# GpSimd takes one row in four of an RMSNorm-SiLU normalization from VectorE

## The chip, the cores and the metric

The kernel runs on one core of a Trainium2 chip. The time is device microseconds (us) of one execution; a median is given with the lowest and highest execution. A *span* is the profiled execution, about 1.3 us shorter than the time. Ratios are the mean time of one kernel's fast runs over the mean of the other's fast runs of the same rounds, so not quite the ratio of the medians quoted beside them. An execution is called slow when it is more than 1.5% above the fastest of the same kernel.

## The reference

```python
# x: 16 x 1024 x 512 float32, gamma: 512 float32 (all ones here), eps 1e-5
rms = np.sqrt(np.mean(x ** 2, axis=-1, keepdims=True) + eps)
x_norm = x / rms * gamma
return x_norm * (1.0 / (1.0 + np.exp(-x_norm)))
```

The input is 33.55 MB and so is the output: 67.1 MB must go through the DMA once.

## The kernel before

The 16,384 rows lie 128 to a partition. A *unit* is four rows of each partition (1 MB in, 1 MB out), and there are 32. Loads are issued by SyncE into a ring of 96 rows per partition; stores are issued by ScalarE. For a unit, ScalarE squares three rows into PSUM and a fourth with a running sum, VectorE sums the three from PSUM, GpSimd makes 1/rms of four numbers per partition, VectorE multiplies each row by 1/rms and gamma in place, and ScalarE applies SiLU in place.

```python
for k in range(K):                                     # GpSimd, 32 units
    aeps[k] = ms[k] + eps          # tensor_scalar, 128x4, waits for the sums of unit k
    rstd[k] = aeps[k] ** -0.5      # tensor_tensor pow, 128x4, waits for aeps
...
def norm(k):                                           # VectorE
    _, at, _ = chunks[k]
    for j in range(cn):                                # cn = 4 rows
        row = xb[:, at + j, :]
        ins = nc.vector.scalar_tensor_tensor(
            out=row, in0=row, scalar=rstd[:, k, j : j + 1], in1=gamma_sb,
            op0=ALU.mult, op1=ALU.mult,
        )
        if j == 0:
            need(ins, s_rstd, k + 1)
    ins.then_inc(s_norm, 1)

for k in range(K + 1):                                 # VectorE's order:
    if k < K:
        sums(k)                                        # tensor_reduce from PSUM
    ...
    if k >= 1:
        norm(k - 1)
```

(The GpSimd loop is written short here; the cuts are marked.)

## Time and profile before

| what | before |
|---|---|
| time, median (lowest to highest) | 160.27 us (160.11 to 160.32) |
| span | 158.7 us |
| one unit in the steady part | 4.31 us |
| VectorE / ScalarE / GpSimd busy | 87% / 79% / 41% |
| DMA rate over the span | 423 GB/s |
| last store issued | 150.11 us |

Read it as two questions. What repeats, and what does one repeat wait for? And does something else stand behind it at nearly the same height? The chain that ended last answers the first only; the DMA in stretches answers the second. The lines themselves are in the prediction below, but for one, the normalizing row (line, operation, shapes, count, then busy us and mean ns of one):

```profile
L224 DVE SCALAR_TENSOR_TENSOR xb<-xb,rstd,gamma_sb 128x512 f32<-128x512 f32 x128 | 87.4, 748 | 0.0
```

### The profile page before, as it was taken

How to read it: one execution, taken by the hardware profiler on the slowest of the kernel's cores; microseconds unless marked ns; L12 is line 12 of the kernel's file. 1: busy time of each engine (PE TensorE's matmuls, PEld its weight loads, DVE VectorE, ACT ScalarE, POOL GpSimd, SP SyncE). 2: the span in 40 equal slices, each digit the busy share in tenths (PEclk: the TensorE clock that was granted, in tenths of full speed). 3: DMA queues.
4: the chain of work that ended last, by engine and by line, in shares of the span. 5: the costliest groups of instructions: out<-in, count | busy, mean ns of one | idle time of the engine just before them, and what ended most of it. 6: DMA issues, size and time to landing. Idle time of an engine off the chain costs nothing.

```text
span 158.7 us, 439 instructions
## 1 busy us (share of the span) xinstructions
DVE 138.9 (87%) x162; ACT 125.3 (79%) x129; POOL 65.4 (41%) x71
## 2 busy tenths in 40 slices
DVE  0249999999999999999999999999999999999300
ACT  0935989888888889988888888888998888883600
POOL 2035444444455555544444445555544444445000
DMA  7999999999999999999999999999999999999997
GB/s 235 427 523 405 396 450 419 409 452 407 460 394 413 467 421 452 413 396 479 432 413 429 446 429 413 425 417 458 429 454 396 434 446 438 446 413 438 388 458 301
DMA packets 3324, 67.15 MB, mean 423 GB/s; under 512 B 501, under 2 KB 501, under 8 KB 505
## 3 DMA queue, kind: packets, MB, share of 16 engines
q1 hardware_dynamic: 1584, 33.56, 49.9%
q10 hardware_dynamic: 1736, 33.57, 49.3%
q14 instruction: 4, 0.02, 0.0%
HBM read 33.56 MB, written 33.56 MB: 423 GB/s over the span
## 4 chain that ended last, share of the span: by engine, by line
DVE 85%; DMA 5%; ACT 1%; issue 1%; POOL 0%; POOLq 0%
DVE xb L224 53%; DVE ms L213 32%; DMA gamma<-in_gamma_dram 5%; ACT xb L184 1%; DVE gamma_sb L237 0%; POOL gamma L142 0%; POOL blank L141 0%; POOLq L65 0%
## 5 line engine op out<-in xcount | busy, mean ns | idle before, releaser
L224 DVE SCALAR_TENSOR_TENSOR xb<-xb,rstd,gamma_sb 128x512 f32<-128x512 f32 x128 | 87.4, 748 | 0.0
L184 ACT ACTIVATE xb<-xb 128x2048 f32<-128x2048 f32 x32 | 61.1, 1909 | 17.8 <-DVE xb L224 17.8
L213 DVE TENSOR_REDUCE ms<-sq 128x3 f32<-128x1536 f32 x32 | 56.1, 1754 | 7.0 <-ACT sq L172 7.0
L147 POOL TENSOR_SCALAR aeps<-ms 128x4 f32<-128x4 f32 x32 | 20.6, 644 | 75.2 <-DVE ms L213 75.2
L172 ACT ACTIVATE sq<-xb 128x1536 f32<-128x1536 f32 x32 | 45.9, 1433 | 0.0
L154 POOL TENSOR_TENSOR rstd<-aeps,neg_half 128x4 f32<-128x4 f32 x32 | 44.0, 1376 | 2.7
L165 ACT ACTIVATE junk<-xb 128x512 bf16<-128x512 f32 x32 | 19.7, 615 | 3.4 <-DMA xb<-in_x_dram 3.3
L165 ACT ACTIVATION_READ_ACCUMULATOR junk<-xb 128x1 f32 x32 | 6.0, 186 | 0.0
L199 ACT ACT_TABLE_LOAD x1 | 1.3, 1283 | 3.6 <-issue 3.6
L237 DVE LOAD_MASK_SELECT gamma_sb<-gamma x1 | 0.0, 14 | 2.3 <-DMA gamma<-in_gamma_dram 2.3
L141 POOL MEMSET blank<- 128x16 f32 x1 | 0.1, 111 | 1.5 <-POOLq L65 1.5
L237 DVE STREAM_SHUFFLE gamma_sb<-gamma 128x512 f32<-128x512 f32 x1 | 0.7, 717 | 0.0
L142 POOL MEMSET gamma<- 128x512 f32 x1 | 0.5, 524 | 0.0
L264 POOL MEMSET const-float32-0.0<- 128x1 f32 x1 | 0.1, 98 | 0.2 <-issue 0.2
L264 POOL MEMSET const-bfloat16-1.0<- 128x1 bf16 x1 | 0.1, 102 | 0.0
L264 POOL MEMSET const-uint8-127<- 128x1 uint8 x1 | 0.1, 101 | 0.0
L143 POOL MEMSET neg_half<- 128x4 f32 x1 | 0.1, 101 | 0.0
L264 POOL MEMSET const-float32-1.0<- 128x1 f32 x1 | 0.1, 98 | 0.0
## 6 DMA issues: line engine op xcount, KB each, us to landing
xb<-in_x_dram SPq DMA_DIRECT2D x6, 4096.0 KB, 41.9
out_dram<-xb ACTq DMA_DIRECT2D x6, 4096.0 KB, 31.1
xb<-in_x_dram SPq DMA_DIRECT2D x3, 2048.0 KB, 35.0
out_dram<-xb ACTq DMA_DIRECT2D x3, 2048.0 KB, 10.7
xb<-in_x_dram SPq DMA_DIRECT2D x2, 1024.0 KB, 5.8
out_dram<-xb ACTq DMA_DIRECT2D x2, 1024.0 KB, 20.8
scratch<-blank ACTq DMA_DIRECT2D x1, 8.0 KB, 7.7
gamma<-in_gamma_dram ACTq DMA_DIRECT2D x1, 8.0 KB
```

Source lines behind the costliest of these rows:

```text
L141: nc.gpsimd.memset(blank, 0.0).then_inc(s_blank, 1)
L142: nc.gpsimd.memset(gamma4, 0.0).then_inc(s_zero, 1)
L147: nc.gpsimd.tensor_scalar(out=aeps[:, k, :], in0=ms[:, k, :], scalar1=eps_f, scalar2=None, op0=ALU.add,),
L154: nc.gpsimd.tensor_tensor(out=rstd[:, k, :], in0=aeps[:, k, :], in1=neg_half, op=ALU.pow),
L165: acc = nc.scalar.activation(out=junk[k % 2], in_=xb[:, at + n_sq, :], func=AF.Square, scale=inv_d**0.5, accum_out=ms[:, k, n_sq : n_sq + 1],)
L172: square = nc.scalar.activation(out=sq[k % 2][:, 0:n_sq, :], in_=xb[:, at : at + n_sq, :], func=AF.Square, scale=inv_d**0.5,)
L184: nc.scalar.activation(out=rows, in_=rows, func=AF.Silu), s_norm, k + 1
L199: nc.scalar.preload_act_table_set("silu_and_others")
L213: nc.vector.tensor_reduce(out=ms[:, k, 0:n_sq], in_=sq[k % 2][:, 0:n_sq, :], op=ALU.add, axis=mybir.AxisListType.X,),
L224: ins = nc.vector.scalar_tensor_tensor(out=row, in0=row, scalar=rstd[:, k, j : j + 1], in1=gamma_sb, op0=ALU.mult, op1=ALU.mult,)
L237: nc.vector.stream_shuffle(gamma_sb, gamma4, [0] * 32), s_gld, 16
L264: nc = _bacc.Bacc("TRN2", target_bir_lowering=False, num_devices=1)
```

## The change

VectorE is busy without a gap and GpSimd is idle for half of the time. The change gives the fourth row of each unit to GpSimd. There it is done with two instructions, one multiply by 1/rms and one by gamma; ScalarE's SiLU waits for both engines. The core of the diff:

```diff
+    n_vec = 3
...
             s_eps, k + 1,
         ).then_inc(s_rstd, 1)
+        if k == 0:
+            nc.gpsimd.wait_ge(s_gamma, 1)
+        _, at, _ = chunks[k]
+        for j in range(n_vec, cn):
+            row = xb[:, at + j, :]
+            done = k * (cn - n_vec) + j - n_vec
+            need(
+                nc.gpsimd.tensor_scalar(
+                    out=row, in0=row, scalar1=rstd[:, k, j : j + 1], scalar2=None,
+                    op0=ALU.mult,
+                ),
+                s_rstd, k + 1,
+            ).then_inc(s_scaled, 1)
+            ins = need(
+                nc.gpsimd.tensor_tensor(out=row, in0=row, in1=gamma_sb, op=ALU.mult),
+                s_scaled, done + 1,
+            )
+        ins.then_inc(s_rest, 1)
...
     def swish(k):
+        nc.scalar.wait_ge(s_rest, k + 1)
...
     def norm(k):
-        for j in range(cn):
+        for j in range(n_vec):
```

More of the change, by code (lines that the diff above doesn't have):

```diff
@@ L95 @@
     s_norm = nc.alloc_semaphore("s_norm")
+    s_rest = nc.alloc_semaphore("s_rest")
+    s_scaled = nc.alloc_semaphore("s_scaled")
     s_swish = nc.alloc_semaphore("s_swish")
```

## The prediction

> **What bounds the kernel now.** I read the page's chain that ended last first, then the windows of DMA share, then the issue-to-landing times of the stores, then the timeline of one steady unit. A unit is four rows per partition, 1 MB in and 1 MB out; there are 32.
>
> ```profile
> DVE 138.9 (87%) x162; ACT 125.3 (79%) x129; POOL 65.4 (41%) x71
> ...
> DMA packets 3324, 67.15 MB, mean 423 GB/s; under 512 B 501, under 2 KB 501, under 8 KB 505
> ...
> DVE 85%; DMA 5%; ACT 1%; issue 1%; POOL 0%; POOLq 0%
> ```
>
> The chain says VectorE: 85% of the span is its two groups, with no idle time between them. Taken alone this promises that taking a quarter of the normalization away saves 32 x 0.66 us = 21 us. But the same page shows 423 GB/s over the whole span, so I looked at the DMA in stretches (columns: stretch and its length, VectorE, ScalarE and GpSimd busy us, clock, DMA share, GB/s):
>
> ```profile
> 4.00:12.00 8.00, 2.72 (x4) 5.04 (x7) 1.26 (x2) 1.00 1.12 471
> 40.00:60.00 20.00, 20.00 (x24) 17.73 (x20) 9.60 (x10) 1.00 1.00 421
> 80.00:100.00 20.00, 20.00 (x24) 17.73 (x19) 8.73 (x10) 1.00 1.01 434
> 120.00:130.00 10.00, 10.00 (x12) 9.10 (x9) 4.10 (x5) 1.00 1.02 441
> 150.00:154.00 4.00, 0.00 (x0) 0.08 (x1) 0.00 (x0) 1.00 1.00 430
> 154.00:158.70 4.70, 0.00 (x0) 0.00 (x0) 0.00 (x0) 1.00 0.77 331
> ```
>
> The DMA share is 1.00 from beginning to end, at about 430 GB/s in every stretch, whether loads and stores are mixed or (after some 110 us) only stores are left. At 430 GB/s the 67.15 MB take 156.2 us of the 158.7. So there are **two walls that stand almost at the same place**: VectorE, and the DMA behind it. Stores show the queue: a 4 MB store needs 31.1 us from issue to landing, though 4.19 MB at 430 GB/s are 9.8 us. At the end, the last silu ends at 150.08, the last store (2.1 MB) is issued at 150.11 and the span ends at 158.7, 8.6 us later. Alone it would take 4.9 us of moving and, by my estimate, some 2 us of issue and completion, 6.8 us. So some 1.8 us of backlog stood before it: the compute may end about 1.8 us later before the span feels it, and if it ends earlier the span gains next to nothing.
>
> One steady unit (start us, length, engine, line, operation), and the first pair of small GpSimd instructions, which ran while VectorE was idle:
>
> ```profile
> 8.87 0.23 POOL L147 TENSOR_SCALAR aeps<-ms 128x4 f32<-128x4 f32 x1 [6.36 <-DVE ms L213]
> 9.18 1.04 POOL L154 TENSOR_TENSOR rstd<-aeps,neg_half 128x4 f32<-128x4 f32 x1
> ...
> 59.11 1.75 DVE L213 TENSOR_REDUCE ms<-sq 128x3 f32<-128x1536 f32 x1
> 59.23 1.91 ACT L184 ACTIVATE xb<-xb 128x2048 f32<-128x2048 f32 x1 [0.45 <-DVE xb L224]
> 60.77 2.73 DVE L224 SCALAR_TENSOR_TENSOR xb<-xb,rstd,gamma_sb 128x512 f32<-128x512 f32 x4
> 60.95 0.66 POOL L147 TENSOR_SCALAR aeps<-ms 128x4 f32<-128x4 f32 x1 [2.19 <-DVE ms L213]
> ...
> 61.69 1.39 POOL L154 TENSOR_TENSOR rstd<-aeps,neg_half 128x4 f32<-128x4 f32 x1
> ```
>
> The unit repeats every 4.31 us: the reduce at 1.67 us of pitch and four normalizing instructions at 0.66 us each (2.65 us). ScalarE needs 1.82 + 0.61 + 1.44 = 3.87 us of it and waits 0.45 us. GpSimd is idle for 2.19 us per unit. The small GpSimd pair takes 0.23 and 1.04 us beside an idle VectorE, 0.66 and 1.39 us beside the normalization.
>
> **What the Trainium skill says, and whether the trace agrees.**
> SBUF — State Buffer, section "Who interferes with whom": VectorE and GpSimd share a read interface; a VectorE instruction with two SBUF inputs contends with a GpSimd instruction that reads SBUF, and the one that came first holds it to its end while the other "fully blocks". The normalization has two SBUF inputs (the row and gamma), the reduce reads PSUM. The trace agrees: the add grows by 0.43 us and the power by 0.35 us, which is what was left of the VectorE instruction in whose midst each began (the first from 60.77 to about 61.43, the second to about 62.1). VectorE's pitch of 0.66 us does not change, as each GpSimd read is only four elements.
> GPSIMD Engine Reference, sections 3.1 and 4.1: a two-input fp32 operation is held to about 2.6 cycles per element (4497 ns for 2048 elements, against 2293 on VectorE), a one-input one is roughly at line rate. The trace before has no such wide read on GpSimd; its write-only memset of 128x512 took 524 ns.
> DMA: Bandwidth & Descriptors, section "Where 436 GB/s comes from": a ceiling of 435 GB/s at the SBUF side, and about 358 from HBM per core with both cores of a pair busy. The measured 430 agrees with the first and exceeds the second, as only one core runs. I take 430 as not to be raised by this change.
>
> **The change part by part.**
> Removed: 32 VectorE instructions at 0.66 us. Unhindered, a VectorE unit falls from 4.31 to 1.67 + 3 x 0.66 = 3.66 us, below ScalarE's 3.87.
> Added on GpSimd: 32 one-input multiplies of 128x512. Estimate: the 0.23 us of the four-element add plus 508 more elements, at one cycle each of 1.2 GHz 0.42 us, so 0.65 us; at the 1.8 cycles that section 3.1 names for a tight loop, 1.0 us. And 32 two-input multiplies. Estimate from 4497 ns for 2048: between 1.12 us (a straight quarter) and 1.27 us (with 0.2 us of it fixed).
> Between GpSimd instructions that wait for one another lie 0.08 us (61.61 to 61.69).
>
> Now the shared interface. When the second multiply of unit k still runs as VectorE wants to begin its three rows, VectorE waits; when it ends, VectorE's first row goes and the next small add waits behind it. I follow GpSimd through one such cycle, from the end of its multiply: the add of the next unit starts together with VectorE's first row and waits it out, 0.63 + 0.17 + 0.08 gap, about 0.9 us; the power falls into the second row as it does today, 1.39 + 0.08 = 1.47 us; the first multiply falls beside the reduce, which is not in its way, 0.65 (to 1.0) + 0.08 us; the second multiply 1.12 to 1.27 us, and no wait after it. The sum is 0.9 + 1.47 + 0.73 + 1.2 = **4.30 us** with the fast first multiply and up to 0.9 + 1.47 + 1.08 + 1.27 = **4.72 us** with the slow one. VectorE has the same cycle: 3.66 us of its own and 0.65 to 1.05 us of waiting for GpSimd at its first row. So the unit becomes bound by a loop of GpSimd and VectorE, no shorter than the 4.31 us of now. My middle is 4.45 us.
>
> At the end: 31 units x (4.45 - 4.31) = 4.3 us later, plus about 0.4 us as the last unit's GpSimd chain (0.9 + 1.5 + 0.7 + 1.2 = 4.3 us and up to two more blocked reads, against 5.31 us of VectorE rows today) is no shorter. Of these 4.7 us the backlog takes 1.8. 160.3 + 2.9 = **163.2**, and since the slow side is the longer one, 163.4 us.
>
> **The rivals.**
> *The DMA floor hides all of it.* If the first multiply is at line rate and the second at 1.12 us, the unit is 4.2 to 4.35 us, the compute ends within 1.8 us of now and the time is 159.8 to 161. In favour: the two walls at one place, and the sum's own lower end of 4.30. Even a unit at ScalarE's 3.87 us would only gain the end's unevenness, 0.5 us or so; faster by 2% would need a span of 155.5 us, 432 GB/s with no start and no tail.
> *VectorE's saving shows in full.* 3.87 us a unit would end the compute near 137 us. The chain of waits speaks for it, the DMA windows against it. It makes 159.8 us, not 140.
> *VectorE wins the interface row after row.* If the second multiply does not hold the interface to its end but is cut into and waits for all three rows, GpSimd carries its 0.31 + 1.12 + 0.73 + 1.2 = 3.4 us and up to 2 us of waiting: 5 us a unit or more, 180 us. Against it: today the small reads do get in between two rows of an unbroken series. One in ten.
> *Slow one-input multiply*, 1.0 us: 4.7 us a unit, 31 x 0.4 + 0.4 - 1.8 = 11 us more, 171 us.
>
> **Range and chances.** The threshold of slower by 2%, 163.5 us, is a unit of 4.46 us, almost my middle. Below it lies the case in which both multiplies are at the good end of their estimates, above it one slow multiply or a wait more. I give 0.52 for slower, 0.46 for the same, 0.02 for faster. The range runs from the DMA floor, 159.0, to the slow multiply, 172.0.
>
> **What the profile after would show.** VectorE busy time falls from 138.9 by some 20 us only if its waits are not counted as busy; if they are, the first row of each three is long, some 1.3 us. GpSimd is busy for nearly the whole unit, near 90% of the span, and the chain that ended last names it and VectorE in turn. The one-input multiply shows 0.65 or 1.0 us, the two-input one 1.1 to 1.3. The DMA share falls below 1 in the last 20 us if the unit is longer than 4.37 us, and stays at 1 until the tail if not. The prediction is wrong if the DMA rate itself changes, if the multiplies cost other than said, or if VectorE's rows do not wait for GpSimd at all.

## The result, and the profile after

The changed kernel takes 177.63 us (177.50 to 177.64, 4 runs) against 160.27 us: a ratio of 1.1083, 95% interval 1.1064 to 1.1103, all fast runs. It is slower by 17.4 us. The prediction had "slower" as its likeliest outcome, but its time and its whole range (159 to 172 us) lie below the result.

From the page of the changed kernel, the lines that answer to the first three shown of before (busy time; DMA; chain by engine):

```profile
DVE 155.5 (88%) x130; ACT 125.2 (71%) x129; POOL 149.0 (85%) x135
...
DMA packets 3324, 67.16 MB, mean 381 GB/s; under 512 B 500, under 2 KB 500, under 8 KB 504
...
POOL 84%; DMA 5%; issue 4%; ACT 1%; DVE 0%; POOLq 0%; ACTq 0%
```

The chain has moved from VectorE to GpSimd. VectorE has 32 instructions fewer and is busy for 16.6 us *more*: its rows last 1133 ns on average in place of 748, so their waiting is counted as busy. The DMA in stretches (columns as before):

```profile
100.00:120.00 20.00, 20.00 (x17) 15.96 (x17) 18.84 (x18) 1.00 1.02 432
...
140.00:150.00 10.00, 10.00 (x9) 7.98 (x10) 9.47 (x9) 1.00 0.00 0
...
165.00:170.00 5.00, 1.19 (x2) 1.91 (x1) 2.23 (x2) 1.00 0.00 0
```

Until 120 us the DMA still runs at 432 GB/s. Then its backlog is used up, and from 140 to 150 us nothing is moved at all: there the DMA is no longer a wall, the compute is. One steady unit of the changed kernel (start us, length, engine, line, operation):

```profile
59.57 0.66 POOL L150 TENSOR_SCALAR aeps<-ms 128x4 f32<-128x4 f32 x1
60.06 1.75 DVE L235 TENSOR_REDUCE ms<-sq 128x3 f32<-128x1536 f32 x1
...
60.31 1.04 POOL L157 TENSOR_TENSOR rstd<-aeps,neg_half 128x4 f32<-128x4 f32 x1
61.45 1.58 POOL L169 TENSOR_SCALAR xb<-xb,rstd 128x512 f32<-128x512 f32 x1
61.73 3.28 DVE L246 SCALAR_TENSOR_TENSOR xb<-xb,rstd,gamma_sb 128x512 f32<-128x512 f32 x3
...
63.11 1.35 POOL L176 TENSOR_TENSOR xb<-xb,gamma_sb 128x512 f32<-128x512 f32 x1
64.44 0.66 POOL L150 TENSOR_SCALAR aeps<-ms 128x4 f32<-128x4 f32 x1
```

GpSimd runs end to end, from one start to the next 0.74 + 1.14 + 1.66 + 1.33 = 4.87 us. The one-input multiply (L169) is the longest of the four. VectorE's three rows take 3.28 us; undisturbed, in e1 below, three take 2.07. One row at a time, for the same unit (duration in ns, start):

```profile
L246 DVE SCALAR_TENSOR_TENSOR xb<-xb,rstd,gamma_sb x1: 948/948/948, 61.7 to 61.7; 128x512 f32<-128x512 f32 x1
...
L246 DVE SCALAR_TENSOR_TENSOR xb<-xb,rstd,gamma_sb x1: 739/739/739, 62.6 to 62.6; 128x512 f32<-128x512 f32 x1
...
L246 DVE SCALAR_TENSOR_TENSOR xb<-xb,rstd,gamma_sb x1: 1748/1748/1748, 63.3 to 63.3; 128x512 f32<-128x512 f32 x1
```

Against the 748 ns of before, the first row, which begins 0.28 us after L169, loses 0.2 us; the third, which meets L176, loses 1.0 us; the one between loses nothing although L169 is still running when it begins. The end of the span follows from the last store: it is issued at 169.34 us in place of 150.11, 19.2 us later, and lands 7.0 us after that in place of 8.6, as no backlog stands before it. 19.2 - 1.6 = 17.6 us, the whole difference of the spans (176.3 - 158.7).

### The profile page after: what moved, and what is told of

It reads as the page before. It is cut to its first block, busy times and chain, and to the rows that moved or that the text cites. A ratio compares the mean times of both kernels' runs of the same rounds, so it can differ in the third digit from the quotient of the medians.

```text
span 176.3 us, 504 instructions
## 1 busy us (share of the span) xinstructions
DVE 155.5 (88%) x130; ACT 125.2 (71%) x129; POOL 149.0 (85%) x135
## 4 chain that ended last, share of the span: by engine, by line
POOL 84%; DMA 5%; issue 4%; ACT 1%; DVE 0%; POOLq 0%; ACTq 0%
POOL xb L169 29%; POOL xb L176 25%; POOL rstd L157 19%; POOL aeps L150 11%; DMA gamma<-in_gamma_dram 5%; ACT xb L206 1%; DVE gamma_sb L259 0%; POOL gamma L145 0%; POOL blank L144 0%; ACTq L204 0%; POOLq L163 0%; POOLq L66 0%
## 5 line engine op out<-in xcount | busy, mean ns | idle before, releaser
L246 DVE SCALAR_TENSOR_TENSOR xb<-xb,rstd,gamma_sb 128x512 f32<-128x512 f32 x96 | 103.8, 1133 | 1.2 <-POOL rstd L157 1.2
L169 POOL TENSOR_SCALAR xb<-xb,rstd 128x512 f32<-128x512 f32 x32 | 51.0, 1594 | 4.9 <-DVE gamma_sb L259 1.8
L176 POOL TENSOR_TENSOR xb<-xb,gamma_sb 128x512 f32<-128x512 f32 x32 | 43.7, 1365 | 2.7
L157 POOL TENSOR_TENSOR rstd<-aeps,neg_half 128x4 f32<-128x4 f32 x32 | 33.5, 1048 | 2.7
```

The lines of the kernel that those rows point to most:

```text
L157: nc.gpsimd.tensor_tensor(out=rstd[:, k, :], in0=aeps[:, k, :], in1=neg_half, op=ALU.pow),
L169: nc.gpsimd.tensor_scalar(out=row, in0=row, scalar1=rstd[:, k, j : j + 1], scalar2=None, op0=ALU.mult,),
L176: nc.gpsimd.tensor_tensor(out=row, in0=row, in1=gamma_sb, op=ALU.mult),
L246: ins = nc.vector.scalar_tensor_tensor(out=row, in0=row, scalar=rstd[:, k, j : j + 1], in1=gamma_sb, op0=ALU.mult, op1=ALU.mult,)
```

## The experiments

**Theories.** (A) GpSimd's one-input multiply costs far more than was estimated, and so GpSimd's loop is too long. (B) GpSimd and VectorE block each other at the shared SBUF interface, and the blocking makes the loop too long. Both may hold; the question is what each is worth. (C) Behind both stands the DMA, so that no repair can be faster than before. Three of the kernels below (e1, run again as e9, e2 and e5) leave out arithmetic on purpose. The comparison with the reference let them pass, presumably because the rows are standard normal and their rms is near one, but as programs they are wrong.

**e1_three_rows**: the saving alone. Kernel before, nobody normalizes the fourth row.

```diff
-        for j in range(cn):
+        for j in range(3):
```

> Kernel before with VectorE normalizing three rows of each unit and nobody the fourth (wrong result on purpose): VectorE's saving without any cost on GpSimd. If the DMA is the floor: the unit falls to ScalarE's 3.87 us, the compute ends about 13 us earlier, the DMA stays at about 430 GB/s to the end, and the time is 159.0 to 160.3 us. If VectorE is the bound, as the chain that ended last says: 160.3 - 31 x 0.44 = 147 us or less.

Measured: a median of 165.76 us, 160.93 to 167.79, 6 runs; the two counted fast are 160.93 and 162.01, ratio 1.0076 (1.0046 to 1.0106). Not one execution gained. The chain of the profiled one, 162.01 us:

```profile
DMA 66%; ACT 11%; DVE 9%; issue 2%; POOL 1%; SPq 0%; ACTq 0%
```

VectorE falls from 85% of the chain to 9%, and the DMA is two thirds of it. Even with a quarter of the normalization thrown away, the time does not fall: theory C holds for this program, and the 21 us that the chain of the kernel before seemed to promise were never there. Both fast executions lie above the 159.0 to 160.3 us expected, and the slow ones were not expected at all; see e9 and e10.

**e2_immediate**: is it the per-partition scalar that is slow?

```diff
-                    out=row, in0=row, scalar1=rstd[:, k, j : j + 1], scalar2=None,
+                    out=row, in0=row, scalar1=1.0, scalar2=None,
```

> Changed kernel with the first GpSimd multiply by the constant 1.0 in place of the per-partition scalar (wrong result on purpose). If the per-partition scalar is what makes this multiply 1.58 us: it falls to about 0.65 us, the unit to 3.95 to 4.3 us, the time to 160 to 161 us. If any one-input multiply of this width costs so on GpSimd: 1.58 us and 177.6 us as before.

Measured: 174.82 us (174.76 to 174.86), ratio 1.0909 (1.0895 to 1.0923). From its steady unit:

```profile
60.55 1.51 POOL L169 TENSOR_SCALAR xb<-xb 128x512 f32<-128x512 f32 x1
```

The multiply takes 1.51 us in place of 1.58, the unit 4.78 us. The per-partition scalar costs 0.07 us of it; the remaining 1.51 us are the multiply itself.

**e3_broadcast**: the same product as a two-input operation, whose second input is 1/rms read with a step of zero.

```diff
-                nc.gpsimd.tensor_scalar(
-                    out=row, in0=row, scalar1=rstd[:, k, j : j + 1], scalar2=None,
-                    op0=ALU.mult,
+                nc.gpsimd.tensor_tensor(
+                    out=row, in0=row,
+                    in1=rstd[:, k, j : j + 1].to_broadcast([P, D]), op=ALU.mult,
```

> Changed kernel with the first GpSimd multiply as a two-input multiply whose second input is rstd read with a step of zero. If a two-input multiply is bound by its two reads, it takes 1.12 to 1.35 us like the gamma multiply, the unit is some 4.6 us and the time about 169 to 170 us. If it is the in-place multiply on GpSimd in itself that costs 1.58 us: 177 us. If the step of zero saves the second read: 0.65 us and 160 us.

Measured: 167.66 us (167.61 to 167.71), ratio 1.0463 (1.0449 to 1.0476). From its steady unit:

```profile
62.15 1.04 POOL L169 TENSOR_TENSOR xb<-xb,rstd 128x512 f32<-128x512 f32 x1
...
63.26 1.27 POOL L176 TENSOR_TENSOR xb<-xb,gamma_sb 128x512 f32<-128x512 f32 x1
...
64.50 0.67 POOL L150 TENSOR_SCALAR aeps<-ms 128x4 f32<-128x4 f32 x1
...
65.25 1.39 POOL L157 TENSOR_TENSOR rstd<-aeps,neg_half 128x4 f32<-128x4 f32 x1
```

The two-input operation does the one-input operation's work in 1.04 us, quicker than the 1.12 to 1.35 us expected (and 167.7 us in place of 169 to 170). The loop is 1.11 + 1.24 + 0.75 + 1.47 = 4.57 us: the saving of 0.55 us is partly given back, because the power now falls beside a row of VectorE and takes 1.39 us again. 10 us of the loss are recovered by this one instruction.

**e4_gamma_psum**: take the supposed cause of blocking away. VectorE reads gamma from an unused slot in PSUM, so that its rows have one SBUF input.

```diff
+            need(
+                nc.vector.tensor_copy(out=sq[0][:, 3, :], in_=gamma_sb), s_gamma, 1
+            ).then_inc(s_gpsum, 1)
...
-                out=row, in0=row, scalar=rstd[:, k, j : j + 1], in1=gamma_sb,
+                out=row, in0=row, scalar=rstd[:, k, j : j + 1], in1=sq[0][:, 3, :],
```

> Changed kernel with VectorE reading gamma from PSUM, so that its rows have one SBUF input and should not meet GpSimd's reads. If blocking at the shared interface makes up the loop: the small add falls from 0.66 to 0.23 us, VectorE's rows are 0.66 us of pitch each without a long one, the unit is 0.31 + 1.12 + 1.66 + 1.2 to 1.43 = 4.3 to 4.5 us, the time 160 to 165 us. If GpSimd's own work alone sets the unit: 4.87 us and 177 us.

Measured: 160.40 us (160.35 to 160.45), ratio 1.0010 (0.9996 to 1.0025). From its steady unit:

```profile
62.58 0.23 POOL L151 TENSOR_SCALAR aeps<-ms 128x4 f32<-128x4 f32 x1
...
62.90 1.04 POOL L158 TENSOR_TENSOR rstd<-aeps,neg_half 128x4 f32<-128x4 f32 x1
63.97 2.06 DVE L247 SCALAR_TENSOR_TENSOR xb<-xb,rstd,sq 128x512 f32<-128x512 f32 x3
64.04 1.57 POOL L170 TENSOR_SCALAR xb<-xb,rstd 128x512 f32<-128x512 f32 x1
...
65.69 1.26 POOL L177 TENSOR_TENSOR xb<-xb,gamma_sb 128x512 f32<-128x512 f32 x1
```

Rows of VectorE and reads of GpSimd now run side by side with no long row and no long add. The loop is 0.32 + 1.14 + 1.65 + 1.23 = 4.34 us, 0.53 us shorter than 4.87: 0.42 us of it in the small add, 0.10 us in the second multiply. The blocking was worth all of the loss of time in the sense that without it the unit is back at the height of the DMA. And the one-input multiply is still 1.57 us here, so its 1.58 us in the steady unit owe nothing to VectorE. (Where it begins in the midst of a row with two SBUF inputs it does grow: to 1.77 us in e7, to 2.13 us in the last unit of the changed kernel.)

**e5_half_width**: what the one-input multiply pays per element.

```diff
-                    out=row, in0=row, scalar1=...
+                    out=row[:, 0 : D // 2], in0=row[:, 0 : D // 2], scalar1=...
```

> Changed kernel with the first GpSimd multiply on the first 256 of the 512 columns only (wrong result on purpose). If it pays for each element, about 2.6 ns: 0.23 + 252 x 2.65 ns = 0.9 us instead of 1.58, the unit 0.68 us shorter, 4.2 us or held by waits at up to 4.5 us, the time 160 to 166 us. If a fixed cost of this kind of instruction makes up the 1.58 us: still above 1.3 us, and 173 us or more.

Measured: 164.84 us, one run with a profile.

```profile
61.36 0.93 POOL L169 TENSOR_SCALAR xb<-xb,rstd 128x256 f32<-128x256 f32 x1
```

256 elements fewer save 1.577 - 0.934 = 0.64 us: 2.5 ns per element and 0.29 us fixed, if two widths make a line. Most of the price is per element. The unit is 4.49 us, at the upper end of what was expected, as the power again falls beside a row (1.38 us).

**e6_not_in_place**: does writing where it reads make it slow? The first multiply writes to a row of its own.

```diff
-                    out=row, in0=row, scalar1=...
+                    out=tmp[k % 2], in0=row, scalar1=...
...
-                nc.gpsimd.tensor_tensor(out=row, in0=row, in1=gamma_sb, op=ALU.mult),
+                nc.gpsimd.tensor_tensor(out=row, in0=tmp[k % 2], in1=gamma_sb, op=ALU.mult),
```

> Changed kernel with the first GpSimd multiply writing to a row of its own, which the second one reads. If writing where it reads is what makes the first multiply slow: it falls to about 0.65 us and the time to 160 to 165 us. If not: 1.58 us, unit 4.87 us, 177.6 us.

Measured: 178.22 us, one run.

```profile
62.10 1.58 POOL L170 TENSOR_SCALAR tmp<-xb,rstd 128x512 f32<-128x512 f32 x1
```

The multiply takes 1.58 us and the unit 4.87 us, as in the changed kernel. In-place is not the cause.

**e7_every_second**: half the dose. GpSimd takes the fourth row of every second unit only.

```diff
+        if k % 2:
+            continue
...
-        for j in range(n_vec):
+        for j in range(cn if k % 2 else n_vec):
```

> Changed kernel with GpSimd taking the fourth row of every second unit only. If GpSimd's amount of work were all that bounds the unit, it has some 7.1 us for two units, VectorE 3.66 + 4.31 = 7.97 us, so 4.0 us a unit, and the DMA floor sets the time: 160 to 161 us (or up to 168, as in the run with three rows). If the waits at the shared interface stay, VectorE has 7.97 + 1.2 us for two units = 4.59 us a unit: about 168 us. If the two-input multiply slips beside the reduce: about 4.2 us a unit and 160 us.

Measured: 164.37 us (164.22 to 164.44), ratio 1.0259 (1.0243 to 1.0274). Two units, one of each kind:

```profile
65.41 1.74 DVE L237 TENSOR_REDUCE ms<-sq 128x3 f32<-128x1536 f32 x1
...
67.01 1.27 POOL L178 TENSOR_TENSOR xb<-xb,gamma_sb 128x512 f32<-128x512 f32 x1
67.07 3.08 DVE L248 SCALAR_TENSOR_TENSOR xb<-xb,rstd,gamma_sb 128x512 f32<-128x512 f32 x3
...
70.07 1.75 DVE L237 TENSOR_REDUCE ms<-sq 128x3 f32<-128x1536 f32 x1
...
71.74 2.72 DVE L248 SCALAR_TENSOR_TENSOR xb<-xb,rstd,gamma_sb 128x512 f32<-128x512 f32 x4
```

This is the plainest line: with GpSimd's multiply beside them, three rows take 3.08 us; alone, four rows take 2.72 us. The row given away saves VectorE 0.66 us and brings it a wait of 1.0 us. The unit with the gift lasts 4.66 us, the one without 4.32 us, together 8.98 us. GpSimd is idle for 1.5 us of each pair here, so it is not too much work on GpSimd that makes this version slower, but the waiting of VectorE. The amount-of-work rival (160 to 161 us) is refuted. The case that held was put at 4.59 us a unit and about 168 us; it is 4.49 us and 164.4.

**e8_psum_broadcast**: both remedies, the edits of e3 and e4 together.

> Changed kernel with both remedies: VectorE reads gamma from PSUM, and the first GpSimd multiply is a two-input one with rstd at a step of zero. GpSimd's loop is 0.32 + 1.14 + 1.11 + 1.24 = 3.81 us, ScalarE's unit 3.87 us, VectorE's 3.66. If compute were the bound: 160.2 - 31 x 0.44 = 147 us. If the DMA is the floor, as the run with three rows said: 160 to 162 us, or up to 168 in some executions, with ScalarE waiting for loads near the end.

Measured: 160.43 us (160.26 to 160.58, 5 runs), ratio 1.0009 (0.9997 to 1.0022). The last store is issued at 144.88 us, 5.2 us earlier than before, and the span is 159.1 us. From its waits (engine, line, waited for: us in total, times, longest):

```profile
ACT junk L187 <- DMA xb<-in_x_dram: 13.0, 5, 6.0
```

The compute now waits 13 us for loads, against 3.3 us before. A unit of 3.87 us in place of 4.31 buys nothing. This version has the fastest compute of those that give the right result, and it ties with the kernel before, as e4 does.

**e9_three_rows_again and e10_psum_broadcast_again**: both fast-computing kernels once more, for the spread of e1.

> The kernel with three rows once more, beside the one with both remedies, on the same chip. If the spread of 160.9 to 167.8 us belongs to this program (a faster compute that crowds stores against loads): again several executions above 163 us. If it was an accident of those runs: all within 160 to 162 us.

> The kernel with both remedies once more. Its compute has the same pace, 3.87 us a unit, as the one with three rows. If the pace of the compute makes the spread, it shows it here too; if it stays at 160.3 to 160.6 us, the pace alone does not make it, and the cause stays open.

Measured: e9 163.54 to 167.97 us (4 runs; the two counted fast are 163.54 and 164.67, ratio 1.0242, 1.0177 to 1.0307, unclear), e10 160.06 to 160.86 us (4 runs, ratio 1.0025, 1.0000 to 1.0050, called unclear too). Two of the seven executions of the kernel before in these rounds were slow as well, 163.63 and 165.07. In the profile of e9, which fell in a slow execution, the last stretch is

```profile
160.00:167.00 7.00, 0.00 (x0) 0.00 (x0) 0.00 (x0) 1.00 0.22 94
```

94 GB/s and a share of 0.22 of 16 engines: the work of three or four DMA engines, as if a few worked on alone while the others had finished; which ones moved data the profile does not show. That is one slow profile; why it meets this program more often than the one of e8 at the same pace stays open. So the 160.9 to 162.0 us of e1 were not seen again. What both runs bear out is only that nothing is gained: no execution of e1 or e9 is below 160.9.

## Why the prediction was wrong

- *What bounds the kernel now: right.* Two walls, VectorE and the DMA behind it. e1 and e8 shorten the unit to 3.87 us, and no median of theirs or of their repeats is below 160.43 us. The rival "VectorE's saving shows in full" was put at 159.8 us; the lowest single execution was 160.06. Two readings were loose: the DMA share also shows 0.91 (12 to 20 us) and 0.92 (145 to 150 us), and loads go on to some 130 us, not 110.
- *The end: right in size.* A last store with nothing before it was estimated at 6.8 us; it took 7.0. The 2 us of issue and completion in that estimate rested on no line of the trace before; afterwards 7.0 - 4.9 = 2.1 us bear them out. The backlog absorbed 1.6 us, said 1.8.
- *The shared interface: right in kind, wrong in place and size.* VectorE's rows do wait for GpSimd's wide reads, but the long one is the third (1.0 us lost), not the first (0.2). The chain that ended last names GpSimd alone (84%, VectorE 0%), not both in turn: VectorE enters the loop only through the 0.53 us that it adds to GpSimd's instructions. The prediction had priced this blocking at 4.30 - 3.36 = 0.94 us (3.36 is its own sum of the same four terms without waits). "No shorter than the 4.31 us of now" came true, but partly by luck: too much blocking made up for a part of the multiply that was priced too low.
- *The sum of the loop, 4.30 us with a middle of 4.45: wrong; it is 4.87.* The term that failed is "the first multiply falls beside the reduce, which is not in its way, 0.65 (to 1.0) + 0.08 us". It did begin beside the reduce, and it still took 1.58 + 0.08 us. I had carried over 0.23 us of the four-element add and put 1 to 1.8 cycles on each further element, the rates that the prediction took from the Trainium skill (GPSIMD Engine Reference, sections 4.1 and 3.1) without a wide read on GpSimd in the trace to check them by. e5 shows 2.5 ns, three cycles of the 1.2 GHz taken there. e2, e4 and e6 show that neither the scalar's form, nor VectorE, nor the place of the result has a large part in it.
- The other three terms against what was measured: add 0.9, measured 0.74; power 1.47, measured 1.14, as the longer loop moved it beside the reduce; second multiply 1.2, measured 1.33. The four errors are -0.16 - 0.33 + 0.93 + 0.13 = +0.57 us, and 4.30 + 0.57 = 4.87. Against the middle of 4.45 the unit is 0.42 us longer, over 31 units 13.0 of the 14.2 us between 163.4 and 177.6.
- *The other signs.* GpSimd was busy for 85% of the span (said near 90%), the second multiply took 1.35 us (said 1.1 to 1.3), VectorE's busy time rose with its waits, and the DMA share fell already between 120 and 140 us (0.94), well before the last 20 us.
- *The last unit: too small.* I gave it 0.4 us. From the first row after the last reduce to the last silu it is 5.42 us before (142.75 to 148.17) and 8.25 us after (159.16 to 167.41), 2.8 us more, as GpSimd was still busy with the unit before. The last reduce itself comes 16.4 us later (30 units, of which the first two were shorter than 4.87). 16.4 + 2.8 = 19.2 us.
- *The slow multiply as a rival: right in direction, too mild.* It was given 1.0 us and 171 us. Since I had widened the estimate only as far as those 1.8 cycles, the range ended at 172.
- *What is shown and what is not.* It is shown that most of the multiply's price is per element and that it is its own, and that the blocking adds 0.53 us to the loop. Neither is the cause alone: the cheaper multiply (e3) recovers 10.0 of the 17.4 us, the end of the blocking (e4) 17.2, and both together (e8) no more than that, as the DMA stands behind. Why this multiply needs three cycles an element, while a two-input one with a step of zero needs 1.04 us for all 512, is not shown by any run.

## What to carry to other kernels

Price work moved to another engine with an instruction of the same kind and width from a trace, or measure it alone first; a four-element instruction (0.23 us here) told little more than the fixed part. Before a busy engine is relieved, see whether the work moved will hold an interface that this engine needs: here a row of 0.66 us was given away for a wait of 1.0 us. And where the DMA runs at its full rate nearly from start to end, expect nothing from rebalancing the engines: here compute that ended 5.2 us earlier (e8) left the time where it was.

## What the Trainium skill lacked or had wrong

- *GPSIMD Engine Reference*, section 4.1, has one-input elementwise work on GpSimd as "roughly line-rate". A multiply of 128x512 by a scalar took 1.58 us (1.51 with a constant), 2.5 ns per element, longer than the two-input multiply beside it (1.35 us; 1.26 us without blocking, in e4).
- The same page, section 3.1, gives about 2.6 cycles per element as the floor of a two-input operation. From that an estimate for 512 elements at the 1.2 GHz of the same section is 1.11 us. With the second input at a step of zero they took 1.04 us in all, a little below it; the page has no row for this case.
- *SBUF — State Buffer*, section "Who interferes with whom", says that the one that came first holds the shared interface for the whole instruction. For the one-input multiply that is not seen: VectorE's first row lost only 0.2 us to it and the second, unhindered at 739 ns, began 0.4 us before the multiply's end. For the two-input multiply it comes near: the row lost 1.0 us of 1.35.
- The same section states that a VectorE instruction with at most one SBUF input does not contend with GpSimd, and e4 agrees. No page was found that draws the remedy from it, to read the second input from PSUM, or says what that costs; here the row took 743 ns with gamma in PSUM and 748 with it in SBUF, and the time fell from 177.6 to 160.4 us.
- *DMA: Bandwidth & Descriptors*, section "Where 436 GB/s comes from", has the HBM side at about 358 GB/s binding for transfers between HBM and SBUF, though it also quotes a measured 425. Here one core alone sustained 393 to 471 GB/s in every stretch of the kernel before from 4 to 154 us, with loads and stores mixed and with stores only. The fault is that section's: other pages of the skill do treat the core that streams alone.
